# A list scheduler orders the second half of an output projection and the up stage, and activation sums are formed in place

## The chip, the cores and the metric

One Trainium2 chip, one of its cores. The time is that of one execution of the program on the device, in microseconds. The core's engines each run their own queue of instructions in order: TensorE (PE; its weight loads are PEld), VectorE (DVE), ScalarE (ACT), GpSimd (POOL), and SyncE (SP), which issues the DMAs.

## The reference

The kernel is one layer of a hybrid decoder block on 1024 positions of width 1024, all in float32: a gated DeltaNet and a sparse attention side by side, a gated merge of the two, and a gated feed-forward part with a depthwise convolution. What the change touches is the end:

```python
m      = sigmoid(gA) * (o_A @ W_A) + sigmoid(gB) * (o_B @ W_B)
h      = LayerNorm(alpha * x + m @ W_out)                # (1024, 1024)
u_g, u_v = split(causal_depthwise_conv3(h @ W_up))       # W_up: 1024 x 5632
f      = (silu(u_g) * u_v) @ W_down                      # W_down: 2816 x 1024
out    = LayerNorm(alpha * h + f)
```

## The kernel before, in words

**Precision.** Each float32 operand of a product is a sum of a high and a low part. The high part is a rounding copy on ACT, the low part the difference, formed on DVE or POOL. A product is high x high, high x low and low x high: three matmuls where one would stand.

**Output projection.** `merge(tt, nh)` computes 128 positions (row block `tt`, 0 to 7) by 512 columns (half `nh`): 24 matmuls into one PSUM bank (`pq`; there are eight). `mT` holds m transposed, high and low, for positions 0 to 511 and 512 to 1023: four tiles, which are the operands of the merges. After the merge, DVE adds alpha * x into `hS` and takes the statistics, POOL raises the variance to the power -1/2, DVE forms the shift, ACT normalises. Then a row block of the first half (tt 0 to 3) is scaled and shifted by four POOL sums (`ln_pool`), one of the second half (4 to 7) by four DVE sums out of PSUM (`ln_psum`, `ln_out`). Then it is stored to DRAM (`hres`), and transposed by eight PE instructions into two banks.

**Up stage.** h @ W_up is done as a 2 x 2 block product with seven products for eight (Strassen's form as Winograd has it). The blocks are positions 0 to 511 and 512 to 1023, depth 0 to 511 and 512 to 1023, and, for column group f (0 to 21), the 128 gate and the 128 value columns. `XB[n]` (n 1 to 7) are the seven sums of activations, high and low. `XB[1]` and `XB[2]` are the two depth halves of positions 0 to 511 (`turn_first`); 3, 5, 6, 7 and 4 come from positions 512 to 1023 and those (`turn_second`: ACT copies and high parts, DVE sums and low parts, POOL two low parts and a sum). They cannot start on a block before it is transposed. `make(f, n)` makes the weights of product n of group f: sums of the raw blocks on POOL, the high part on ACT, the low part on POOL. `Group.run(n)` is the product, 12 matmuls; `Group.after(n)` what follows on ACT and DVE: sums of products (`u`), the convolution's three taps into `accs`, and in `gate` the tanh form of silu and the product with the value half. The result is stored (`gdr`).

**What sets the order.** In this part of the program the order on every engine is the one in which the instructions are written (`manual_schedule`). The tiles of `XB[1]` and `XB[2]` take slots of a pool of six that the first projection half's weights free; `XB[3]`, 5, 6 and 7 take four that are free once the last merge has read `mT`. So the second half's sums start when all merges are over. Four groups (0 to 3) run products 1 and 2 ahead, one group between each of the transpositions 4 to 7, while the others are formed. From then on a table sets the steps: products 6, 7, 5, 4, 3 for the first four groups, 1, 6, 7, 5, 2, 4, 3 for the rest, weights made up to eight products ahead in a ring of ten tiles.

**Down stage.** For each half of the positions, four row blocks with two banks each. The first `KF` = 4 of 22 depth tiles go to row blocks 0 and 1, then to 2 and 3, so that the second pair of banks is wanted later; then tile by tile, and the last six row block by row block, each ending in the second LayerNorm.

Of the kernel before, what the change touches and what calls it, by code (L numbers as in the profile page):

```python
# [25 lines left out]
LNLAG = 2  # L26
# [24 lines left out]
def hybrid_block_kernel(ctx: ExitStack, tc: tile.TileContext, x, w_in, gdn_conv_w, gdn_a_log,  # L51
# [997 lines left out]
    def merge(tt, nh):  # L1049
        hf, o = tt // 4, (tt % 4) * 128  # L1050
        hs = HS[nh]
        who, wlo = wo[nh]
        ps = pq()
# [5 lines left out]
        V.scalar_tensor_tensor(hrow(tt)[:, hs], hrow(tt)[:, hs], ALPHA, ps, op0=OP.mult, op1=OP.add)  # L1059

    def turned(tt):
        ps = [pq(), pq()]
        for k in range(KT):
            PE.transpose(ps[k // 4][:, (k % 4) * 128:(k % 4 + 1) * 128], hrow(tt)[:, k * 128:(k + 1) * 128], ident)
        return [p.rearrange("p (k c) -> p k c", k=4) for p in ps]

    def turn_first(tt):
        o = slice(tt * 128, tt * 128 + 128)
        ps = turned(tt)
        for n, pv in zip((1, 2), ps):  # L1070
            A.activation(XB[n][:, 0, :, o], pv, AF.Copy)
        for n, pv in zip((1, 2), ps):
            V.tensor_tensor(XB[n][:, 1, :, o], pv, XB[n][:, 0, :, o].bitcast(F32), op=OP.subtract)

    def turn_second(tt):
        o = slice((tt - 4) * 128, (tt - 4) * 128 + 128)
        p12, p22 = turned(tt)

        def part(n, i):
            return XB[n][:, i, :, o]  # L1080

        def tmp():
            return ff.tile([128, 512], F32, name="tb", tag="tb", bufs=4).rearrange("p (k c) -> p k c", k=4)

        def hi(n, src):
            A.activation(part(n, 0), src, AF.Copy)

        def lo(n, src, eng):
            eng.tensor_tensor(part(n, 1), src, part(n, 0).bitcast(F32), op=OP.subtract)

        t3, t4 = tmp(), tmp()
        A.activation(t3, p12, AF.Copy)
        hi(3, p22)
        V.tensor_tensor(p12, p12, part(1, 0).bitcast(F32), op=OP.subtract)
        V.tensor_tensor(p12, p12, part(1, 1).bitcast(F32), op=OP.subtract)
        A.activation(t4, p12, AF.Copy)
        V.tensor_tensor(t3, p22, t3, op=OP.subtract)
        lo(3, p22, V)
# [5 lines left out]
        V.tensor_tensor(t4, p22, part(2, 0).bitcast(F32), op=OP.subtract)
# [342 lines left out]
```

## Time and profile before

| | us |
|---|---|
| median of 3 runs | 1816.57 (1814.01 to 1817.13) |
| the profiled execution | 1816.3 |
| its span in the profile | 1814.6 |
| PE busy in the span | 1720.6 (95%) |
| DVE, ACT, POOL busy | 1070.5, 726.1, 822.3 |
| PE busy in 1020 to 1200 us (180 us) | 127.94 |
| PE busy in 1200 to 1520 us (320 us) | 318.84 |

A row of a group gives the line in the kernel, engine, operation, output<-inputs, shape and count, then busy time and mean ns of one, then the time the engine stood idle just before such instructions and what ended it. A row of a timeline begins with the start and the duration in us; "x12" are twelve instructions merged into one row. The chain of waits is the work that ended last, followed back. All matmuls, of merges, products and the down stage, stand on one line (L97), and are told apart by their tiles: `woh`, `wol` with `mT` in the merges, `xb` with `wb` in the up stage, `wd` with `gs` in the down stage.

### The profile page before, as it was taken

Reading aid. Unit: us, or ns where it says so; the run is one execution under the profiler, and the core shown is the slowest. Engines: PE = TensorE matmul, PEld = TensorE weight load, DVE = VectorE, ACT = ScalarE, POOL = GpSimd, SP = SyncE. Lnnn points to the kernel's source line nnn. Section 1 sums busy time; section 2 is a strip of 40 time slices with the busy share of each in tenths; the row PEclk is TensorE's granted clock in tenths of the full one; section 3 lists DMA queues with packets and bytes.
Section 4 is the critical chain, followed back from the end, with each engine's and each line's share of the span. In section 5 each row is a group of like instructions: output and inputs, shape, how many; then the busy total and the mean of one; then the engine's idle time right before and its main releaser. Section 6 shows DMA issues by size and latency. Waiting matters only on the chain.

```text
span 1814.6 us, 23297 instructions
## 1 busy us (share of the span) xinstructions
PE 1720.6 (95%) x8710; PEld 1444.7 (80%) x8710; DVE 1070.5 (59%) x2048; ACT 726.1 (40%) x1282; POOL 822.3 (45%) x609
## 2 busy tenths in 40 slices
PE   8999999999999999999899965799999999899997
PEld 8888888888888788888687854578888888688886
DVE  3567767576625388898633264386666666613624
ACT  3323323222224488888531033244444444431421
POOL 1322222222214244444672244777777776654731
PEclk9999999999999999999999987899999999899999
DMA  5222122222213000000256021233223222763521
GB/s 168 71 83 61 45 69 56 58 60 72 83 47 96 25 1 1 1 1 7 87 186 232 12 93 47 59 104 92 71 82 93 81 82 99 285 225 110 175 92 47
DMA packets 158382, 152.38 MB, mean 84 GB/s; under 512 B 16392, under 2 KB 129213, under 8 KB 158269
## 3 DMA queue, kind: packets, MB, share of 16 engines
q1 hardware_dynamic: 158269, 150.89, 26.4%
q8 instruction: 69, 1.13, 0.3%
q14 instruction: 44, 0.36, 0.1%
HBM read 119.67 MB, written 31.20 MB: 83 GB/s over the span
## 4 chain that ended last, share of the span: by engine, by line
PE 83%; DVE 6%; POOL 4%; ACT 3%; issue 2%; DMA 1%; SPq 0%; POOLq 0%; DVEq 0%; ACTq 0%
PE pq L97 35%; PE big L97 32%; PE sm L97 12%; PE sm L852 3%; POOL wb L1173 1%; DVE accs L1193 1%; POOL h L1139 1%; POOL h L1138 1%; ACT P L817 1%; DVE gs L1374 0%; DVE st L815 0%; DMA w<-in_w_down_dram 0%; DVE wl L855 0%; ACT wb L1172 0%; POOL tb L1161 0%
## 5 line engine op out<-in xcount | busy, mean ns | idle before, releaser
L97 PE MATMUL pq<-xb,wb 128*128 128x512 f32 x1848 | 430.9, 395 | 48.4 <-ACT u L1216 37.8
L97 PEld LDWEIGHTS pq<-xb,wb 128*128 128x128 f32 x1848 | 352.3, 191 | 125.3 <-ACT u L1216 39.3
L87 POOL TENSOR_TENSOR wl<-w,wh 128x1024 fp32r<-128x1024 f32 (+2 forms) x51 | 122.5, 2407 | 361.4 <-PE big L97 130.2
L97 PE MATMUL big<-xTl,wh 128*128 128x512 f32 x624 | 249.9, 401 | 0.0
L97 PE MATMUL big<-xTh,wh 128*128 128x512 f32 x624 | 249.7, 400 | 0.0
L97 PE MATMUL pq<-wd,gs 128*128 128x512 f32 x1056 | 243.1, 392 | 6.1 <-DVE accs L1246 4.0
L97 PEld LDWEIGHTS pq<-wd,gs 128*128 128x128 f32 x1056 | 199.8, 189 | 49.1 <-DVE accs L1246 5.1
L1193 DVE SCALAR_TENSOR_TENSOR accs<-pq,fcw,accs 128x511 f32<-128x511 f32 (+3 forms) x264 | 144.9, 569 | 87.7 <-ACT accs L1196 83.2
L97 PE MATMUL big<-xTh,wl 128*128 128x512 f32 x624 | 163.7, 398 | 0.0
L779 POOL TENSOR_TENSOR P<-P,st 128x640 f32<-128x640 f32 (+7 forms) x96 | 99.8, 1067 | 126.6 <-DVE st L788 61.1
L1173 POOL TENSOR_TENSOR wb<-w,wb 128x512 fp32r<-128x512 f32 x88 | 113.2, 1293 | 80.4 <-ACT wb L1172 79.7
L1366 POOL TENSOR_TENSOR wd<-w,wd 128x1024 fp32r<-128x1024 f32 x44 | 110.7, 2537 | 70.5 <-ACT wd L1365 70.5
L97 PEld LDWEIGHTS big<-xTl,wh 128*128 128x128 f32 x624 | 117.6, 188 | 20.9 <-issue 0.2
L97 PEld LDWEIGHTS big<-xTh,wh 128*128 128x128 f32 x624 | 117.6, 189 | 20.8
L97 PEld LDWEIGHTS big<-xTh,wl 128*128 128x128 f32 x624 | 113.9, 188 | 22.0
L1196 ACT ACTIVATE accs<-pq,fcw 128x512 f32<-128x512 f32 x88 | 59.9, 684 | 163.1 <-PE pq L97 80.9
L1374 DVE TENSOR_TENSOR gs<-gr,gs 128x512 fp32r<-128x512 f32 x44 | 57.9, 1327 | 91.7 <-ACT gs L1373 91.6
L855 DVE TENSOR_TENSOR wl<-sm,wh 128x512 fp32r<-128x512 f32 (+1 forms) x148 | 99.6, 683 | 11.3 <-ACT wh L854 8.9
L86 ACT ACTIVATE wh<-w 128x1024 fp32r<-128x1024 f32 (+2 forms) x51 | 53.1, 1047 | 127.2 <-PE big L97 85.7
L854 ACT ACTIVATE wh<-sm 128x512 fp32r<-128x512 f32 (+1 forms) x148 | 87.1, 594 | 27.9 <-PE sm L852 24.1
L97 PE MATMUL big<-kS,qS 128*128 128x512 f32 (+3 forms) x384 | 89.0, 350 | 3.0 <-DVE qS L631 3.0
L817 ACT ACTIVATE P<-big,st 128x640 f32<-128x640 f32 (+7 forms) x128 | 88.6, 699 | 6.6 <-DVE st L815 6.1
(344 smaller groups left out, 3200.9 us busy)
## 6 DMA issues: line engine op xcount, KB each, us to landing
w<-in_w_down_dram SPq DMA_DIRECT2D x44, 512.0 KB, 3.8
w<-in_w_in_dram SPq DMA_DIRECT2D x40, 512.0 KB, 4.2
w<-in_w_up_dram SPq DMA_DIRECT2D x36, 512.0 KB, 3.9
gdr<-accs SPq DMA_DIRECT2D x22, 512.0 KB, 2.6
gr<-gdr SPq DMA_DIRECT2D x44, 256.0 KB, 3.6
sig<-th SPq DMA_DIRECT2D x32, 256.0 KB, 2.4
w<-sig SPq DMA_DIRECT2D x16, 512.0 KB, 3.3
wx<-in_w_up_dram SPq DMA_DIRECT2D x11, 512.0 KB, 5.2
```

The source lines that it names most:

```text
L87: G.tensor_tensor(wl[:, :n], w[:, :n], wh[:, :n].bitcast(F32), op=OP.subtract)
L97: PE.matmul(o, a, b, start=start, stop=stop, skip_group_check=True)
L779: G.tensor_tensor(p, p, r.to_broadcast([128, p.shape[1]]), op=OP.mult)
L817: A.activation(P[:, r0 + i, :n], pv[:, i], AF.Exp, bias=nm[:, i:i + 1], accum_out=su[:, i:i + 1])
L852: PE.transpose(tp[:n, r * 128:(r + 1) * 128], P[:, r, c0:c0 + n], ident)
L854: A.activation(ph, tp[:n], AF.Copy)
L855: V.tensor_tensor(pl, tp[:n], ph.bitcast(F32), op=OP.subtract)
L1173: G.tensor_tensor(w[:, 1], src, w[:, 0].bitcast(F32), op=OP.subtract)
L1193: V.scalar_tensor_tensor(o, i, fcw[:, 2 - s, j:j + 1], o, op0=OP.mult, op1=OP.add)
L1196: A.activation(acc[:, HS[h]], p, AF.Copy, scale=fcw[:, 2, j:j + 1])
L1366: G.tensor_tensor(o[:, 1], w, o[:, 0].bitcast(F32), op=OP.subtract)
L1374: V.tensor_tensor(g[:, 1], r, g[:, 0].bitcast(F32), op=OP.subtract)
```

## The change

A scheduler is added to the kernel: each piece of work is a node with an engine (or two to choose from, with a duration each), nodes that it depends on, and tokens that it takes and gives (banks, ring tiles, raw tiles, temporaries). PE's merges and products have a fixed order (`seq`); from their times each node gets a latest start; then time is stepped, each free engine taking the ready node with the earliest. The nodes are emitted in that order.

With it: the second half of the projection runs the row blocks as 0, 4, 1, 5, 2, 3, 6, 7; `XB[1]`, 2, 6 and 7 are the `mT` tiles themselves, a block's columns being overwritten when its merge has read them; the temporaries of the sums are a pool of 3 (before: 4), with one tile apart for a weight sum; the low parts of the weights of groups 0 to 2, and the weight sums of groups 0 and 1, may go to DVE; a row block of h is stored in one DMA instead of two; and `KF` is 6.

```diff
+class Plan:
+    LAT = {"PE": .25, "A": .15, "V": .15, "G": .15, "S": 1.6, "X": 0}
...
+            for e in free:
+                if free[e] > t + 1e-9:
+                    continue
+                for n in todo[e]:
...
+                    if any(d.end is None or d.end + d.lat > t + 1e-9 for d in n.deps):
+                        continue
+                    if any(len(self.pools[p]) < n.take.count(p) for p in n.take):
+                        continue
...
+                    n.start, n.dur = t, n.engs[e]
+                    n.end = free[e] = t + n.dur
...
-    def xblock(n, pool):
-        XB[n] = pool.tile([128, 2, 4, 512], F32R, name=f"xb{n}", tag="s")
+    for n, (q, hf) in {1: ("h", 0), 2: ("l", 0), 6: ("h", 1), 7: ("l", 1)}.items():
+        XB[n] = mT[q, hf].rearrange("p (i k) c -> p i k c", i=2)
+    for n in (3, 5):
+        XB[n] = S6.tile([128, 2, 4, 512], F32R, name=f"xb{n}", tag="s")
...
+    P.pool("bank", 8)
+    P.pool("ring", tokens=["wh", "wl", "wh", "wl"])
+    P.pool("raw", tokens=["w", "w", "w"])
+    P.pool("tmp", 3)
...
+    ORDER = (0, 4, 1, 5, 2, 3, 6, 7)
...
+        merged[tt] = P.add("PE", 5.45, m, [prev], take=["bank"], seq=True)
+        n = P.add("V", 2.3, st, [merged[tt]], take=["ag"], give=[(merged[tt], "bank")])
+        w = P.add("G", .5, lambda _: ln_pow(s["ag"]), [n])
+        w = P.add("V", .16, lambda _: ln_shift(s["ag"]), [w])
...
+        turned[tt] = P.add("PE", 1.05, t_, outs + [merged[tt]], take=["bank", "bank"], prio=-30)
...
+        D12 = add("V", 1.3, d12, [t, f1, A1])
+        A3 = add("A", .5, a3, [D12], take=["tmp"])
+        H5 = add("A", .5, hi(5, tt, p12), [D12])
+        D3 = add("V", .6, lambda _: V.tensor_tensor(t3(), p22(), t3(), op=OP.subtract), [A1])
...
+        L7 = add({"G": 1.25, "V": .65}, None, lo(7, tt, t3), [H7], give=[(A1, "tmp")])
...
+        L4 = add({"G": 1.25, "V": .65}, None, lo(4, tt, t4), [H4], give=[(A3, "tmp")])
...
+        fast = {"G": 1.25, "V": .65} if f < 3 else "G"
...
+        H = P.add("A", .53, h_, deps + [chain["make"]], take=["ring"], node=True)
...
+        L = P.add(fast, 1.25, l_, [H], give=list(give))
...
+            e = {"G": 1.25, "V": .65} if f < 2 else "G"
...
+            self.s1 = P.add(e, 1.25, s1, [w1, w2, chain["sum"]], take=["sum"], node=True)
+            self.s2 = P.add(e, 1.25, s2, [self.s1] + wait, take=["tmp"], node=True)
...
+            deps = [W[f, n][1]] + xdone[n] + ([] if free else [chain["prod"]])
+            deps += {2: [self.n.get("u1")], 4: [self.n.get("u2")], 3: [self.n.get("c22")]}.get(n, [])
+            p = self.n[n] = P.add("PE", 2.724, p_, deps, take=["bank"] if head else [],
+                                  give=[(W[f, n][0], "ring")], seq=True)
...
+    for g in groups[:AHEAD]:
+        g.run(1, True)
+        g.run(2, True)
...
+    order = P.run()
...
+        with tc.manual_schedule(engines=ME):
+            for n in part:
+                n.emit()
...
-    KL, KF = 6, 4
+    KL, KF = 6, 6
```

**PE, from the end of the merges to product 6 of group 0.** `h_9096` are row blocks 0 to 3, `h_9097` blocks 4 to 7; `x8` is one block's transposition; `mTh_8479` and `mTl_8480` are the mT tiles of the first half of the positions, in the changed kernel also `XB[1]` and `XB[2]`; `xb_9340` and `xb_9341` are `XB[1]` and `XB[2]` before. Before:

```order
L97 MATMUL pq<-xb_9340,wb 128x512 x12
L1064 MATMUL pq<-ident,h_9097 128x128 x8
L97 MATMUL pq<-xb_9341,wb 128x512 x12
L1064 MATMUL pq<-ident,h_9097 128x128 x8
L97 MATMUL pq<-xb_9340,wb 128x512 x12
L97 MATMUL pq<-xb_9341,wb 128x512 x12
L1064 MATMUL pq<-ident,h_9097 128x128 x8
```

And now, from the last matmul of merge 6 (the 23 matmuls between the first and the last of merge 7 are left out):

```order
L191 MATMUL pq<-woh_9322,mTl_8482 128x512
L1252 MATMUL pq<-ident,h_9096 128x128 x8
L1252 MATMUL pq<-ident,h_9097 128x128 x8
L191 MATMUL pq<-woh_9322,mTh_8481 128x512
...
L191 MATMUL pq<-woh_9322,mTl_8482 128x512
L1252 MATMUL pq<-ident,h_9096 128x128 x8
L191 MATMUL pq<-mTh_8479,wb 128x512 x24
L1252 MATMUL pq<-ident,h_9097 128x128 x16
L191 MATMUL pq<-mTl_8480,wb 128x512 x24
L191 MATMUL pq<-mTh_8479,wb 128x512 x24
L191 MATMUL pq<-mTl_8480,wb 128x512 x24
L191 MATMUL pq<-mTh_8481,wb 128x512 x12
```

Transpositions 2 and 5 stand between merges 6 and 7, 3 behind merge 7, 6 and 7 together behind two products; before, each of 4 to 7 had one or two products around it.

**DVE, from merge 7's residual to the low parts of block 3.** L1151 is the residual, L1177 to L1187 the statistics and the shift, L1309, L1311 and the `xb_9341` row pieces of block 5's sums, the last two rows the low parts of block 3 for `XB[1]` and `XB[2]`:

```order
L1151 SCALAR_TENSOR_TENSOR h_9097<-h_9097,pq 128x512
L1177 BN_STATS bs<-h_9097 128x6
L1187 SCALAR_TENSOR_TENSOR ag<-ag 128x1
L1309 TENSOR_TENSOR pq<-pq,tb 128x512
L1267 TENSOR_TENSOR xb_9341<-pq,xb_9341 128x4x128
L1177 BN_STATS bs<-h_9097 128x6
L1179 BN_AGGR ag<-bs 128x2
L1180 TENSOR_SCALAR ag<-ag 128x1
L1311 TENSOR_TENSOR tb<-pq,mTl_8480 128x512
L1267 TENSOR_TENSOR mTh_8479<-pq,mTh_8479 128x4x128
L1267 TENSOR_TENSOR mTl_8480<-pq,mTl_8480 128x4x128
```

Before, the low parts of block 3 stood behind merge 5's statistics, and merge 7's residual behind the four sums of row block 6.

**DVE, between the sums and group 0's first product sum.** Before, `u` (L1219) came directly behind the sums' low parts (L1089):

```order
L1089 TENSOR_TENSOR xb_9753<-pq,xb_9753 128x4x128
L1089 TENSOR_TENSOR xb_9752<-pq,xb_9752 128x4x128
L1219 TENSOR_TENSOR u<-pq,u 128x512
L1222 TENSOR_TENSOR u<-pq,u 128x512
L1224 TENSOR_TENSOR pq<-pq,u 128x512
```

Now there stand between them low parts and sums of weights (L1371, L1422, L1427) and the taps of groups 0 and 1 (L1382):

```order
L1267 TENSOR_TENSOR xb_9807<-tb,xb_9807 128x4x128
L1382 SCALAR_TENSOR_TENSOR accs<-pq,fcw,accs 128x510
L1371 TENSOR_TENSOR wb<-tb,wb 128x512
L1382 SCALAR_TENSOR_TENSOR accs<-pq,fcw,accs 128x511
L1371 TENSOR_TENSOR wb<-wx,wb 128x512
L1371 TENSOR_TENSOR wb<-sb,wb 128x512
L1382 SCALAR_TENSOR_TENSOR accs<-pq,fcw,accs 128x510
L1371 TENSOR_TENSOR wb<-w,wb 128x512
L1422 TENSOR_TENSOR tb<-sb,w 128x512
L1427 TENSOR_TENSOR w<-w 128x512
L1371 TENSOR_TENSOR wb<-tb,wb 128x512
L1480 TENSOR_TENSOR u<-pq,u 128x512
```

The weight rows were POOL's before; they have both operands in SBUF (`w`, `wx`, `tb`, `sb`, `wb`).

More of the change, by code (lines that the diff above doesn't have):

```diff
@@ L1058, in merge @@
             mm(ps, ml, who[:, k, :], False, k == KT - 1)
[L1059 to L1073, printed above, removed]
@@ new lines, in residual @@
+    def residual(ps, tt, nh):
+        o = hrow(tt)[:, HS[nh]]
+        V.scalar_tensor_tensor(o, o, ALPHA, ps, op0=OP.mult, op1=OP.add)
+    with tc.manual_schedule(engines=MS):
+        for tt in range(NT):
+            ps = pq()
+            merge(ps, tt, 0)
+            residual(ps, tt, 0)
+        for k in range(0, KT, 2):
+            load_out(1, k, wtile())
+    for n, (q, hf) in {1: ("h", 0), 2: ("l", 0), 6: ("h", 1), 7: ("l", 1)}.items():
+        XB[n] = mT[q, hf].rearrange("p (i k) c -> p i k c", i=2)
@@ new lines, in hybrid_block_kernel, with hi, lo, turn_first @@
+    for tt in ORDER:
+        rows(tt)
+    last_merge = merged[ORDER[-1]]
+    xdone = {n: [] for n in range(1, 8)}
+    def hi(n, tt, src):
+        return lambda _: copy(xpart(n, 0, tt), src())
+    def lo(n, tt, src):
+        return lambda e: e.tensor_tensor(xpart(n, 1, tt), src(), xpart(n, 0, tt).bitcast(F32), op=OP.subtract)
+    first = {}
+    def turn_first(tt):
+        s = state[tt]
+        for i, n in enumerate((1, 2)):
+            a = P.add("A", .5, hi(n, tt, lambda i=i: s["p"][i]), [turned[tt]])
+            first[tt, n] = P.add("V", .6, lo(n, tt, lambda i=i: s["p"][i]), [a], give=[(turned[tt], "bank")])
+            xdone[n].append(first[tt, n])
@@ L1178, in product, with tile_u, taps @@
+    def tile_u():
+        return ff().tile([128, 512], F32, name="u", tag="u", bufs=5)
+    def taps(acc, p0, p1, j, part, s):
+        o, i = {"0": (acc[:, s:512], p0[:, :512 - s]), "1": (acc[:, 512 + s:], p1[:, :512 - s]) if p1 is not None
+                else None, "s": (acc[:, 512:512 + s], p0[:, 512 - s:])}[part]
+        V.scalar_tensor_tensor(o, i, fcw[:, 2 - s, j:j + 1], o, op0=OP.mult, op1=OP.add)
+    def product(o, f, n, start, stop):
+        w = W[f, n][0].tile
         for k in range(4):
@@ new lines, in after @@
+                N["sa"] = scaled(0, "a", 0, f, [N[2], chain.get("acc", None)], take=["acc"])
+                N["ta"] = tap(0, "a", None, f, "0", [N["sa"]])
+                c = scaled(1, "c", 1, NFF + f, [N["c22"], N["sa"]])
+                c21 = P.add("V", .6, lambda _: V.tensor_tensor(t["b"], t["u3"], t["b"], op=OP.subtract), [p, N["u3"]],
+                            give=[(N["u3"], "u")])
+                b = scaled(1, "b", 0, NFF + f, [c21, N["sa"]])
+                x = tap(1, "b", "c", NFF + f, "1", [c], [(N[7], "bank")])
@@ new lines, in hybrid_block_kernel @@
+    groups = [Group(f) for f in range(NFF)]
+    for g in groups[:AHEAD]:
+        g.weights(0)
+    for f, g in enumerate(groups):
+        if f >= AHEAD:
+            g.weights(0)
+        g.weights(1)
+    for g in groups[:AHEAD]:
+        g.run(1, True)
+        g.run(2, True)
+    chain["prod"] = groups[AHEAD - 1].n[2]
+    for f, g in enumerate(groups):
+        for n in ([6, 7, 5, 4, 3] if f < AHEAD else [1, 6, 7, 5, 2, 4, 3]):
+            g.run(n)
+    order = P.run()
+    cut = next(i for i, n in enumerate(order) if n is opened)
```

537 lines of the change are left out of this document (311 added, 226 removed).

## The prediction, on record before the changed kernel was run

> **What bounds the kernel now.** I read the page's busy shares and chain first, then TensorE's groups stage by stage, then the places where it stood still.
>
> ```profile
> PE 1720.6 (95%) x8710; PEld 1444.7 (80%) x8710; DVE 1070.5 (59%) x2048; ACT 726.1 (40%) x1282; POOL 822.3 (45%) x609
> ...
> PE 83%; DVE 6%; POOL 4%; ACT 3%; issue 2%; DMA 1%; SPq 0%; POOLq 0%; DVEq 0%; ACTq 0%
> ```
>
> TensorE (PE) sets the end nearly everywhere; the 17% of the chain on other engines is what a reordering can win. These are groups of the windows 990 to 1200 us (two rows), 1200 to 1520 and 1500 to 1815:
>
> ```profile
> L97 PE MATMUL pq<-xb,wb 128*128 128x512 f32 x286 | 76.4, 429 | 47.3 <-ACT u L1216 37.8 <-DVE accs L1193 7.6 <-DVE pq L1224 1.3
> L1064 PE MATMUL pq<-ident,h 128*128 128x128 f32 x64 | 8.8, 275 | 4.8 <-DVE xb L1073 4.3 <-POOL h L1139 0.5
> L97 PE MATMUL pq<-xb,wb 128*128 128x512 f32 x1407 | 319.3, 389 | 1.2 <-DVE pq L1224 1.2
> L97 PE MATMUL pq<-wd,gs 128*128 128x512 f32 x1056 | 243.1, 392 | 6.1 <-DVE accs L1246 4.0 <-DVE accs L1193 2.1
> ```
>
> The up stage's products run without a gap from 1200 us on (319.3/1407 = 0.227 us per matmul, 2.72 us per product of 12); nearly all waiting lies in its first 286 matmuls. The changed stretch on PE, in time; brackets give the idle time before a row and what ended it:
>
> ```profile
> 1061.32 0.80 PE L97 MATMUL pq<-woh,mTh 128*128 128x512 f32 x1
> ...
> 1064.47 0.46 PE L97 MATMUL pq<-wol,mTh 128*128 128x512 f32 x1
> ...
> 1073.87 2.89 PE L97 MATMUL pq<-xb,wb 128*128 128x512 f32 x12
> ...
> 1092.02 4.54 PE L97 MATMUL pq<-xb,wb 128*128 128x512 f32 x12 [14.39 <-ACT u L1216]
> ...
> 1105.83 4.47 PE L97 MATMUL pq<-xb,wb 128*128 128x512 f32 x12 [5.63 <-ACT u L1216]
> ...
> 1123.22 4.32 PE L97 MATMUL pq<-xb,wb 128*128 128x512 f32 x12 [9.31 <-ACT u L1216]
> ...
> 1128.17 2.98 PE L97 MATMUL pq<-xb,wb 128*128 128x512 f32 x12
> 1139.63 20.94 PE L97 MATMUL pq<-xb,wb 128*128 128x512 f32 x84 [8.48 <-ACT u L1216]
> 1168.15 22.01 PE L97 MATMUL pq<-xb,wb 128*128 128x512 f32 x84 [7.58 <-DVE accs L1193]
> ```
>
> By the group rows PE stood idle 47.3 us before products and 4.8 before transpositions (L1064), 52.1 in all. After a long wait it is slow: between 1061.32 and 1064.47, behind the wait of 4.3, seven matmuls took 3.15 us instead of 1.59, 1.6 lost; the blocks of 12 behind a wait took 4.54, 4.47 and 4.32 instead of 2.89, 4.7 lost; the blocks of 84 took 20.94 and 22.01 instead of 19.2, 4.5 lost. Together **62.9 us** that a better order could win here.
>
> Why they arise shows in the chain: each transposed row block goes through ACT, DVE and POOL while PE's next product stands behind it in PE's own queue.
>
> ```profile
> 1025.47 0.69 DVE h L1059
> ...
> 1042.57 0.52 POOL ag L293
> 1043.31 1.25 ACT h L1136
> 1044.63 1.30 POOL h L1138
> 1046.00 1.29 POOL h L1139
> 1047.29 1.26 POOL h L1138
> 1048.62 1.27 POOL h L1139
> 1049.89 0.52 POOL ag L293
> ```
>
> One row block of the first half costs a POOL-paced 7.3 us (1042.57 to 1049.89) against 5.45 us for its merge on PE (24 x 0.227). Four in a row, as now, fall behind PE. A block of the second half uses DVE instead (four sums, 2.6 us at L1104's price below).
>
> **The change, part by part.**
>
> *Merges 0, 4, 1, 5, 2, 3, 6, 7 instead of 0 to 7.* Nothing is added on PE: the same 192 matmuls and 64 transposes. Alternation gives POOL two merges per expensive block for the first three. I followed the new queues with the rows above: merge 0 ends at 1025.2 (L1059 reads it at 1025.47); its rows are ready at 1035.2 as now, and PE reaches transposition 0 at 1036.1. Transpositions 4, 1, 5, 2 and 3 have rows ready at about 1042.4, 1046.5, 1056.6, 1060 and 1067.4, and PE comes at 1042.7, 1049.2, after 1061, 1061 and 1068.7. No wait; the smallest margins, 0.3 and 0.9 us, may each cost a few tenths.
>
> *Sums in place over mT.* This is what allows it: XB1, 2, 6 and 7 need no tile that only frees after the last merge, so the second-half sums of blocks 4 and 5 are formed during the merges. It adds no instruction.
>
> *First product after transposition 3.* Here I find a new wait. DVE's queue holds, between the end of merge 7 and the low part of XB1 for block 3, merge 7's residual and statistics, a shift and three pieces of block 5. Their prices:
>
> ```profile
> 1069.05 1.29 DVE L1073 TENSOR_TENSOR xb<-pq,xb 128x512 fp32r<-128x512 f32 x2 [2.07 <-ACT xb L1071]
> ...
> 1080.22 1.28 DVE L1114 BATCH_NORM_STATS2 bs<-h 128x6 f32<-128x512 f32 x2
> ...
> 1088.78 0.69 DVE L1104 TENSOR_TENSOR tb<-pq,xb 128x512 f32<-128x512 f32 x1 [0.66 <-ACT xb L1086]
> ```
>
> 0.2 hop, 0.6 residual, 1.2 statistics, 0.6 for three tiny rows, three sums at 0.65, one low part 0.6: 5.2 us, of which the transposition covers 0.9. PE waits 4.3 us, and as after the 4.3 us of now loses 1.6 more to the clock. Bounds: 2 us, if the hops overlap, to 6.
>
> *Products 1 and 2 of four groups, with transpositions 6 and 7 between them in one place.* The four pairs no longer stand behind one transposition each: what PE did between 1073.87 and 1131.1 in pieces is 8 x 2.72 = 21.8 us in one run. Block 7 leaves DVE about 0.4 us after PE wants it: 0.4.
>
> *Weight sums and low parts on DVE for the first three groups.* The plan prices such a row at 0.65 us on DVE. The trace does not: with both operands in SBUF and POOL working beside it, DVE was slower, with one operand in PSUM it was not. (The first row gives min/median/max in ns.)
>
> ```profile
> L1374 DVE TENSOR_TENSOR gs<-gr,gs x44: 670/890/2892, 1535.4 to 1751.0; 128x512 fp32r<-128x512 f32 x44
> L919 DVE TENSOR_TENSOR oAl<-gA,oAh 128x512 fp32r<-128x512 f32 x4 | 5.4, 1385 | 0.0
> L855 DVE TENSOR_TENSOR wl<-sm,wh 128x512 fp32r<-128x512 f32 x132 | 89.0, 684 | 8.6 <-ACT wh L854 6.6
> L1173 POOL TENSOR_TENSOR wb<-w,wb 128x512 fp32r<-128x512 f32 x88 | 113.2, 1293 | 80.4 <-ACT wb L1172 79.7
> ```
>
> I take 1.3 us per such row while POOL is at its own sums (bounds 0.67 and 1.55; L919 is nearest, since POOL's rows are 1.3 us there too). [...]
>
> Where that falls: count from the end of transposition 7. PE has 6 products before group 0's product 6, so it comes to product 4 of group 0 after 9 x 2.72 = 24.5 us. Product 4 needs DVE's u2. In DVE's queue ahead of it stand 17 sums of blocks 6 and 7 (11.1 us at 0.65), 9 two-SBUF rows (11.7), 4 taps (2.6) and u2 itself (0.7) with hops (0.8): 27 us. PE waits **2.5**, then 0.4 for the sum that frees bank d. The backlog of some 6 us passes to group 1, whose product 5 needs group 0's bank b: **3.3**. I add 0.9 for the clock. [...] Groups 2 and 3 then have DVE free enough: a group needs
>
> ```profile
> 1200.00:1520.00 320.00, 318.84 (x1407) 263.74 (x1406) 214.20 (x362) 138.35 (x237) 234.44 (x186) 1.00 0.27 84
> ```
>
> (columns: PE, PE load, DVE, ACT, POOL) 214.2 x 19.05/320 = 12.8 us of DVE against 13.6 of PE with five products.
>
> *Groups 4 to 21.* Ring of ten weight tiles, makes per group, lead and the order of loads and gate stores are as before within one instruction. I price it at 0: PE's own 19.05 us per group cover POOL's 14.2 (11 rows at 1.29) and DVE's 12.8. Three temporaries for four and one sum tile cost nothing as long as POOL's chain stays inside that.
>
> *Down stage, six tiles first instead of four.* Now:
>
> ```profile
> 1558.60 8.77 PE L97 MATMUL pq<-wd,gs 128*128 128x512 f32 x38
> 1569.51 1.38 PE L97 MATMUL pq<-wd,gs 128*128 128x512 f32 x3 [2.14 <-DVE accs L1193]
> 1574.85 25.41 PE L97 MATMUL pq<-wd,gs 128*128 128x512 f32 x100 [3.96 <-DVE accs L1246]
> 1561.76 1.06 ACT L1365 ACTIVATE wd<-w 128x1024 fp32r<-128x1024 f32 x1 [5.05 <-DMA w<-in_w_down_dram]
> ```
>
> PE runs out of banks until the last group's gate is through (6.1 us), then is slow (25.41 for 100 against 22.9: 2.5). Two more tiles on the first two row blocks are 24 matmuls, 5.45 us of other work in that wait. Their loads pass through the same ACT queue in which the gate's scaling already stood behind a load (the 5.05), so the gate may come later by as much: bounds 0 and 8.6. I take 5.5.
>
> *Tail.* The last row block's chain is the same instructions: 0.
>
> **Sum.** Lost now 62.9. Lost after: 4.3+1.6+0.4+2.5+0.4+3.3+0.9 = 13.4. Won 49.5 here and 5.5 in the down stage, 55. The profiled execution took 1816.3 us (span 1814.6 and 1.7 around it; the runs' median is 1816.57, 0.3 above): 1816.3 - 55 = **1761**.
>
> [...]
>
> **The rivals.**
>
> - *DVE and POOL hardly collide* (POOL often waits for ACT): only the wait after transposition 3 stays, 62.9 - 6.3 + 5.5 = 62 won, 1754. For it: POOL stood idle 79.7 us for ACT in the L1173 row. Against: in this stretch POOL has its own backlog.
> - *DVE becomes the bound of the first four groups.* 12.8 of 13.6 us leaves it nothing to catch up with, and groups 1 and 2 still get two-SBUF rows; groups 2 and 3 then lose some 5.5 each, and the result is 1772.
> - *Slower:* the weight chain bounds groups 4 to 21. With one sum tile, a group's first sum waits for the last one's two-term weights; POOL's 14.2 us and the ACT hops between its rows would have to come to more than 19.05 + 55/18 = 22.1 us per group to turn the gain into a loss; at 23, 1761 + 18 x 3.95 = 1832. Against: now the same rows fit, with PE idle 1.2 us in 320.
> - *The change doesn't move what waits.* The queues show that it does: one product pair per transposition before, none after.
>
> **How the numbers follow.** My forecast 0.48, no collision 0.20, DVE bound 0.24, slower 0.05, no change 0.03. The least that the bounds give is 1749 (no collision, 8.6 in the down stage), the most of the first three about 1778 (waits at their upper bounds, nothing in the down stage). The range 1750 to 1777 holds them and leaves out the last two and the tails. A measurement of this kernel can tell 0.2% (3.6 us) from no change; faster 0.93, same 0.02, slower 0.05.
>
> **What would show it.** Right: PE without a wait over 1 us from merge 0 to transposition 3; one of some 4 us before the first product, ended by DVE's low part of XB1; waits of 2 to 4 us in groups 0 and 1, ended by DVE; two-SBUF rows of DVE at 1 us or more there; PE gapless from group 4 on; about 4 us less idle at the first bank wait of the down stage. Wrong: a transposition late by several us, gaps in every group after the fourth, or the first down tiles late on PE ahead of the last two products.

## The result, and the profile after

The changed kernel takes 1762.66 us (median of four runs, 1758.11 to 1763.04) where the kernel before takes 1816.11 on the same chip: 0.9701 of the time, 95% interval 0.9683 to 0.9720. The forecast was 1761, with a range of 1750 to 1777. The profiled execution took 1762.67 us. From its page, the busy shares, the chain of waits and three groups of PE:

```profile
PE 1719.1 (98%) x8710; PEld 1440.8 (82%) x8710; DVE 1100.4 (62%) x2068; ACT 732.2 (42%) x1282; POOL 804.8 (46%) x589
...
PE 85%; DVE 6%; issue 3%; ACT 2%; POOL 2%; DMA 1%; DVEq 0%; POOLq 0%; ACTq 0%; SPq 0%
...
L191 PE MATMUL pq<-wd,gs 128*128 128x512 f32 x1056 | 241.5, 391 | 0.4 <-DVE accs L1513 0.4
...
L191 PE MATMUL pq<-xb,wb 128*128 128x512 f32 x792 | 189.0, 393 | 2.6 <-DVE accs L1382 2.1
...
L191 PE MATMUL pq<-mTh,wb 128*128 128x512 f32 x528 | 127.3, 397 | 3.2 <-ACT mTh L1172 3.1
```

The products now read `mTh` and `mTl` as well as `xb`, since four of the seven sums lie there. Before, 47.3 us of idle time stood ahead of the products; now 2.6 and 3.2. All that PE waits for between 1000 and 1200 us (engine, tile and line of the waiting row, what it waited for, us in total, times, longest):

```profile
PE pq L191 <- ACT mTh L1172: 3.1, 1, 3.1
PE pq L191 <- DVE accs L1382: 2.1, 1, 2.1
PE pq L191 <- DVE pq L1485: 0.5, 1, 0.5
PE pq L1252 <- DVE h L1241: 0.3, 1, 0.3
```

In the windows view (PE, PE load, DVE, ACT, POOL, clock) PE is without a gap from 1145 to 1500 us:

```profile
1145.00:1500.00 355.00, 355.00 (x1559) 292.40 (x1558) 234.16 (x398) 160.12 (x264) 253.12 (x197) 1.00 0.27 86
```

In the timeline, two blocks behind waits show the slow clock, and the last row is the down stage, 330 matmuls without a wait:

```profile
1078.36 8.73 PE L191 MATMUL pq<-mTh,wb 128*128 128x512 f32 x24 [3.08 <-ACT mTh L1172]
...
1127.55 10.03 PE L191 MATMUL pq<-xb,wb 128*128 128x512 f32 x36 [2.10 <-DVE accs L1382]
...
1514.75 75.42 PE L191 MATMUL pq<-wd,gs 128*128 128x512 f32 x330
```

At 0.227 us each, and 0.16 more for the last, 24 matmuls take 5.6 us and 36 take 8.3; so 3.1 and 1.7 us went to the clock.

**A measure that leaves out what comes before.** Three tiles mark three points: `woh` the first matmul of the projection, `wb` the last product of the up stage, `wd` the last of the down stage (duration min/median/max in ns, then first and last start). Before, and after:

```profile
L97 PE MATMUL pq<-woh,mTh x128: 389/389/796, 976.2 to 1073.2; 128*128 128x512 f32 x128
L97 PE MATMUL pq<-xb,wb x1848: 387/389/796, 1073.9 to 1558.4; 128*128 128x512 f32 x185
L97 PE MATMUL pq<-wd,gs x1056: 388/389/796, 1550.2 to 1804.3; 128*128 128x512 f32 x176
```

```profile
L191 PE MATMUL pq<-woh,mTh x128: 387/389/496, 982.0 to 1073.6; 128*128 128x512 f32 x128
L191 PE MATMUL pq<-xb,wb x792: 388/389/628, 1110.8 to 1514.5; 128*128 128x512 f32 x198
L191 PE MATMUL pq<-wd,gs x1056: 388/389/503, 1504.1 to 1750.8; 128*128 128x512 f32 x176
```

From the first projection product to the last up product it was 582.2 us and is 532.5 (49.7 won); from there to the last down product 245.9 and 236.3 (9.6 won). But the first projection product comes 5.8 us later than before: 49.7 + 9.6 - 5.8 + 0.1 of the tail = 53.6, the difference of the two profiled executions (1816.3 - 1762.67). (Some 2 us of down products have moved ahead of the last up product, 10.4 us of overlap against 8.2, so the border between the first two numbers is soft by that much.) The same three points in all profiles of this study, one profile per kernel (the last column is the median of several runs; the kernel before, run beside each batch, had medians of 1814.78 to 1816.12):

| kernel | first projection product at | to last up product | to last down product | median of the runs |
|---|---|---|---|---|
| before | 976.2 | 582.2 | 245.9 | 1816.11 |
| changed | 982.0 | 532.5 | 236.3 | 1762.66 |
| changed, again | 980.2 | 532.6 | 236.3 | 1761.14 |
| late sums | 980.2 | 533.4 | 239.3 | 1764.71 |
| rows in turn | 979.6 | 534.1 | 237.0 | 1761.99 |
| KF 4 | 982.5 | 532.7 | 242.2 | 1766.32 |
| weights on POOL only | 982.3 | 529.4 | 236.3 | 1757.15 |
| block 3 first | 980.9 | 532.1 | 236.6 | 1761.23 |
| POOL only and block 3 first | 981.0 | 532.7 | 236.4 | 1760.76 |
| three freedoms taken back | 978.8 | 531.9 | 237.4 | 1760.23 |
| and PE's queue as before | 977.6 | 534.2 | 239.8 | 1765.05 |
| before, product 1's copy first | 974.3 | 568.4 | 243.3 | 1799.78 |
| and scaling ahead of weights | 975.7 | 566.8 | 244.5 | 1799.20 |
| before, KF 6 | 974.8 | 583.8 | 236.8 | 1808.74 |

### The profile page after: what moved, and what is told of

It is laid out like the page before. It is cut to its first block, busy times and chain, and to the rows that moved or that the text cites. A ratio compares the mean times of both kernels' runs of the same rounds, so it can differ in the third digit from the quotient of the medians.

```text
span 1761.0 us, 23301 instructions
## 1 busy us (share of the span) xinstructions
PE 1719.1 (98%) x8710; PEld 1440.8 (82%) x8710; DVE 1100.4 (62%) x2068; ACT 732.2 (42%) x1282; POOL 804.8 (46%) x589
## 3 DMA queue, kind: packets, MB, share of 16 engines
q8 instruction: 69, 1.13, 0.3%
## 4 chain that ended last, share of the span: by engine, by line
PE 85%; DVE 6%; issue 3%; ACT 2%; POOL 2%; DMA 1%; DVEq 0%; POOLq 0%; ACTq 0%; SPq 0%
PE pq L191 35%; PE big L191 33%; PE sm L191 13%; PE sm L946 3%; ACT P L911 1%; DVE st L909 1%; DVE wb L1371 1%; DVE accs L1382 0%; DVE wl L949 0%; POOL h L1228 0%; POOL h L1229 0%; DMA w<-in_w_out_dram 0%; PE big L245 0%; DVE gs L1573 0%; DVE oAl L1013 0%
## 5 line engine op out<-in xcount | busy, mean ns | idle before, releaser
L191 PE MATMUL pq<-xb,wb 128*128 128x512 f32 x792 | 189.0, 393 | 2.6 <-DVE accs L1382 2.1
L1382 DVE SCALAR_TENSOR_TENSOR accs<-pq,fcw,accs 128x510 f32<-128x510 f32 (+3 forms) x264 | 145.8, 569 | 63.3 <-ACT accs L1466 58.1
L191 PEld LDWEIGHTS pq<-xb,wb 128*128 128x128 f32 x792 | 149.7, 189 | 35.6 <-ACT wb L1172 2.5
L191 PE MATMUL pq<-mTh,wb 128*128 128x512 f32 x528 | 127.3, 397 | 3.2 <-ACT mTh L1172 3.1
L191 PE MATMUL pq<-mTl,wb 128*128 128x512 f32 x528 | 127.4, 391 | 0.0
L191 PEld LDWEIGHTS pq<-mTh,wb 128*128 128x128 f32 x528 | 100.8, 191 | 25.7 <-ACT mTh L1172 3.3
L1371 POOL TENSOR_TENSOR wb<-w,wb 128x512 fp32r<-128x512 f32 x79 | 102.8, 1302 | 37.8 <-ACT wb L1172 37.8
L191 PEld LDWEIGHTS pq<-mTl,wb 128*128 128x128 f32 x528 | 99.1, 188 | 21.2
L1573 DVE TENSOR_TENSOR gs<-tb,gs 128x512 fp32r<-128x512 f32 x44 | 71.4, 1641 | 67.0 <-ACT gs L1572 64.2
L949 DVE TENSOR_TENSOR wl<-sm,wh 128x512 fp32r<-128x512 f32 (+1 forms) x148 | 99.8, 684 | 13.7 <-ACT wh L948 11.3
```

The costliest lines, as they stand in the source:

```text
L191: PE.matmul(o, a, b, start=start, stop=stop, skip_group_check=True)
L949: V.tensor_tensor(pl, tp[:n], ph.bitcast(F32), op=OP.subtract)
L1371: e.tensor_tensor(H.tile[:, 1], src(), H.tile[:, 0].bitcast(F32), op=OP.subtract)
L1382: V.scalar_tensor_tensor(o, i, fcw[:, 2 - s, j:j + 1], o, op0=OP.mult, op1=OP.add)
L1573: V.tensor_tensor(g[:, 1], r, g[:, 0].bitcast(F32), op=OP.subtract)
```

## The experiments

**The kernel again.** Nothing edited.

> The changed kernel once more, unedited. In its first profile the output projection's first product began at 981.99 us, 5.8 us later than before's (976.16), after a stretch from 880 to 900 us in which the granted clock was 0.66 and 0.83 where before had 0.99 and 1.00, though the code up to there is the same. Theory: that delay belongs to the run and not to the change, so another execution may begin the projection between 976 and 982, and its time is between 1757 and 1763. Rival: the change itself delays this stretch (its code or buffers lie elsewhere); then the first product begins at 982 again within 1 us.

1761.14 us (1759.48 to 1762.88), ratio 0.9704 (0.9688 to 0.9720). From the first projection product to the last up product ("the stretch" from here on) it repeats to 0.1 us. The projection began at 980.2 us, which by the bounds set above is the theory and not the rival. But the table has fourteen profiles: without the scheduler the projection begins at 974.3 to 976.2 (four), with it at 977.6 to 982.5 (ten). The two groups do not overlap, although ahead of the projection every engine's instructions are the same ones in the same order. So it is not only the run, as I had it; what in the change causes it, no run tells.

**Sums behind the last merge.**

```diff
+        after = last_merge
...
-        A1 = add("A", .5, a1, [t], take=["tmp"])
-        H3 = add("A", .5, hi(3, tt, p22), [t])
+        A1 = add("A", .5, a1, [t, after], take=["tmp"])
+        H3 = add("A", .5, hi(3, tt, p22), [t, after])
```

> The sums of row blocks 4 to 7 may start only after the last merge; all else stays. Theory: blocks 4 and 5 have their sums done beneath the merges in the changed kernel; put behind them, they give DVE about 2 blocks x 10 rows x 0.65 = 13 us more behind the last merge, where DVE is nearly full (26.9 of 30 us from 1070 to 1100), so the products that need the second half come 8 to 13 us later and 1 to 3 us go to the clock: 1771 to 1779. Rival: the eight products 1 and 2 that go first (8 x 2.72 = 21.8 us of TensorE) cover this; then the time stays within 2 us of the changed kernel's.

1764.71 us, ratio 0.9726 (0.9712 to 0.9741), 0.9 us more in the stretch, and 3.0 more in the down stage, for which I have no reason. The theory, 8 to 13, is wrong: the products 1 and 2 of four groups cover the sums. The rival, within 2 us, holds for the stretch; the whole is 2.1 and 3.6 us above the two medians of the changed kernel. That the sums can be formed during the merges was, by the prediction, what allowed the gain; in the stretch it is worth about 1 us.

**Row blocks in turn.**

```diff
-    ORDER = (0, 4, 1, 5, 2, 3, 6, 7)
+    ORDER = (0, 1, 2, 3, 4, 5, 6, 7)
```

> The row blocks are merged in the order 0 to 7 instead of 0, 4, 1, 5, 2, 3, 6, 7. Blocks 0 to 3 are normalised by POOL (4 rows x 1.29 = 5.2 us each) and 4 to 7 by DVE (4 rows x 0.69 = 2.8 us each, and 10 rows of sums). Theory: the interleaving is what keeps both engines level with a merge of 5.45 us; in turn, POOL is full for four blocks while DVE waits, and DVE then has four blocks of about 12 us one behind the other, which ends some 6 to 15 us later than now: 1768 to 1778. Rival: the order hardly matters, since TensorE's merges bound both halves: within 2 us of the changed kernel.

1761.99 us, ratio 0.9708 (0.9694 to 0.9723), 1.6 us more in the stretch and the whole as before the edit. The theory of 6 to 15 falls. PE's waits are more and shorter, none over 2.2 us.

**KF back to 4, and KF 6 alone in the kernel before.**

```diff
-    KL, KF = 6, 6
+    KL, KF = 6, 4
```

> Four products instead of six of the first pair of the down stage run ahead (KF 4, as before). Theory: the 7.9 us saved at the start of the down stage come from the two more products of 2 x 1.9 us that fill the waits for banks, so 5 to 8 us come back: 1767 to 1771. Rival: it was the order of the last groups' sums, which frees the banks earlier; then 0 to 2 us.

> The kernel before with KF 6 instead of 4 and nothing else. The changed kernel with KF 4 took 5.2 us more. Theory: the same 24 matmuls fill the same waits here, 4 to 6 us won: 1809 to 1811. Rival: in before the first waits of the down stage stand behind the loads of its first tiles, which wait for slots that the last groups still hold; then it is within 2 us of before.

KF 4 in the changed kernel: 1766.32 us, ratio 0.9734 (0.9719 to 0.9748), just below the theory's 1767; 5.9 us more behind the last up product. The waits for banks are back, in its timeline:

```profile
1526.68 0.97 PE L191 MATMUL pq<-wd,gs 128*128 128x512 f32 x3 [2.94 <-DVE accs L1513]
1528.01 62.18 PE L191 MATMUL pq<-wd,gs 128*128 128x512 f32 x264 [0.36 <-DVE accs L1513]
```

KF 6 alone in the kernel before: 1808.74 us, ratio 0.9959 (0.9945 to 0.9974), 7.3 us less than before's 1816.02 beside it, where 4 to 6 were expected; in the down stage it is 9.1 us less (245.9 to 236.8). There its down stage runs on without any wait:

```profile
1558.78 31.42 PE L97 MATMUL pq<-wd,gs 128*128 128x512 f32 x136
```

So this number alone is enough to save the time in the down stage. It is not the only way: the changed kernel with KF 4 has 242.2 us there, 3.7 less than before's 245.9. The loads that come ahead of the gate in ACT's queue, for which I had allowed up to 5 us, cost nothing that shows.

**All weight rows on POOL.**

```diff
-        fast = {"G": 1.25, "V": .65} if f < 3 else "G"
+        fast = "G"
...
-            e = {"G": 1.25, "V": .65} if f < 2 else "G"
+            e = "G"
```

> The sums and low parts of weights all go to POOL, as before the change; in the plan as it is, 17 of the rows that may go either way are DVE's and would now be POOL's. Theory: 17 rows of 1.29 us are 22 us more for POOL while DVE gives up about 17 x 1.1; POOL has 46 us idle in 1020 to 1145, but the rows are wanted within the first three groups, so 4 to 12 us are lost against the changed kernel: 1766 to 1774. Rival: the collision of the two engines costs as much as the help brings (DVE rows at 1.1 to 1.8, POOL rows at 1.64 to 1.75 instead of 1.29); then it is level or 2 to 4 us faster: 1758 to 1762.

1757.15 us, ratio 0.9679 (0.9665 to 0.9694): the rival, a little below even its 1758, and the lowest median here. The ratio's interval still overlaps the changed kernel's, so the whole time does not settle it; but the stretch is 3.1 us shorter, where the unedited kernel repeats to 0.1, and the 2.1 us wait for bank b is gone. Groups of the window 1090 to 1145, in the changed kernel:

```profile
L1371 POOL TENSOR_TENSOR wb<-wx,wb 128x512 fp32r<-128x512 f32 x3 | 4.3, 1421 | 2.0 <-ACT wb L1172 1.9
L1371 DVE TENSOR_TENSOR wb<-sb,wb 128x512 fp32r<-128x512 f32 x3 | 4.3, 1417 | 0.0
L1422 POOL TENSOR_TENSOR tb<-sb,w 128x512 f32<-128x512 f32 x2 | 3.5, 1731 | 0.0
L1371 DVE TENSOR_TENSOR wb<-w,wb 128x512 fp32r<-128x512 f32 x3 | 3.2, 1070 | 0.0
...
L1371 DVE TENSOR_TENSOR wb<-tb,wb 128x512 fp32r<-128x512 f32 x3 | 2.5, 841 | 0.1
L1371 DVE TENSOR_TENSOR wb<-wx,wb 128x512 fp32r<-128x512 f32 x2 | 2.5, 1232 | 0.0
```

and with POOL alone:

```profile
L1371 POOL TENSOR_TENSOR wb<-w,wb 128x512 fp32r<-128x512 f32 x9 | 11.6, 1291 | 0.0
L1371 POOL TENSOR_TENSOR wb<-sb,wb 128x512 fp32r<-128x512 f32 x4 | 5.2, 1298 | 0.0
```

A low part of weights takes DVE 1.13 us on average in eleven rows (4.3 + 3.2 + 2.5 + 2.5 us), not the 0.65 of the plan, while POOL's rows become 1.42 and 1.73 instead of 1.29. (Not every slow POOL row comes from the help: with POOL alone, too, one row of L1422 takes 1.74, beside DVE's own low parts of the activations.) Alone, POOL works without idle time in these groups and is in time. The help held up taps that PE was waiting for. Both engines pay here: beside POOL's rows, from 1102.84 to 1109.3 us, DVE's rows with both operands in SBUF took 1.12, 1.13, 1.79 and 1.34 us, and the next three, while POOL stood idle (1108.77 to 1111.27), 0.68, 0.68 and 0.69; in the means of these groups a POOL row was 0.43 us at most above the 1.30 of its low parts without the help.

**Block 3 ahead of norm 6, and this with POOL alone.** In the changed kernel ACT's queue at the first product was:

```profile
1075.83 1.49 ACT L1190 ACTIVATE pq<-h,ag 128x512 f32<-128x512 f32 x2 [0.75 <-DVE ag L1187]
1077.25 1.05 ACT L1172 ACTIVATE mTh<-pq 128x512 fp32r<-128x512 f32 x2
```

```diff
-                z = P.add("A", .72, z_, [w], take=["bank"], ...)
+                z = P.add("A", .72, z_, [w] + ([turned[3]] if tt == 6 else []), take=["bank"], ...)
...
-            a = P.add("A", .5, hi(n, tt, ...), [turned[tt]])
+            a = P.add("A", .5, hi(n, tt, ...), [turned[tt]], prio=-40 if tt == 3 else 0)
```

(and the same `prio` for the two low parts on DVE.)

> In the changed kernel ACT normalises row block 6 only when transposition 3 is through, and the two copies of block 3 and DVE's two low parts of it go ahead of all else there. Theory: the wait of 3.1 us ahead of the first product is norm 6 (1.49 us) and one weight row standing ahead of the copies; it falls to about 1.5, and of the 3.1 us lost to the clock after it most goes: 3 to 5 us faster than the changed kernel, 1757 to 1759. Rival: norm 6 coming later moves the wait to transposition 6: no change within 1.5 us.

1761.23 us, ratio 0.9697 (0.9683 to 0.9712): as the changed kernel. Its timeline on PE:

```profile
1074.98 0.49 PE L191 MATMUL pq<-mTh,wb 128*128 128x512 f32 x1 [0.85 <-ACT mTh L1172]
1077.54 7.14 PE L191 MATMUL pq<-mTh,wb 128*128 128x512 f32 x23 [2.06 <-DVE mTh L1267]
```

The wait for the copy falls from 3.08 to 0.85 us, and now the second matmul waits 2.06 us for the low part on DVE, the wait that the prediction had named; in the changed kernel it was covered by the ACT copy. Block 6, held back, then makes its transposition wait. One place was three waits deep.

> The two edits of the changed kernel together that looked useful: all weight rows on POOL, and block 3's copies and low parts ahead of norm 6 and of all else. Theory: the first took away the wait of 2.1 us for bank b and the slow clock after it (3.1 us less up to the last up product), the second only turned one wait of 3.1 and its slow clock into five short ones; together 528 to 530 from the first projection product to the last up product, 1755 to 1759 in all. Rival: they share one wait, and the shorter waits at the transpositions delay the weights: 1760 to 1763.

1760.76 us, ratio 0.9697 (0.9684 to 0.9710): the rival. The two edits do not add up: the stretch takes 532.7 us, and POOL alone had 529.4. The transpositions of the last blocks wait four times, 3.0 us in all (2.3 with block 3 first alone), and the 24 matmuls behind them take 7.64 us where 5.6 is usual:

```profile
1088.89 7.64 PE L191 MATMUL pq<-mTl,wb 128*128 128x512 f32 x24
```

So POOL alone paid in one kernel and not in this one.

**The copy of product 1 ahead of the sums, in the kernel before.** By now neither the order of the rows nor the early sums had explained 50 us. In before, ACT's queue between the first two products was, from 1082 us on:

```profile
1082.86 1.48 ACT L1126 ACTIVATE pq<-h,ag 128x512 f32<-128x512 f32 x2 [5.23 <-DVE ag L1119]
1084.28 0.57 ACT L1092 ACTIVATE tb<-pq 128x512 f32<-128x512 f32 x1
1084.76 0.58 ACT L1086 ACTIVATE xb<-pq 128x512 fp32r<-128x512 f32 x1
1086.35 0.60 ACT L1096 ACTIVATE tb<-pq 128x512 f32<-128x512 f32 x1 [1.02 <-DVE pq L1095]
1086.94 0.63 ACT L1086 ACTIVATE xb<-tb 128x512 fp32r<-128x512 f32 x1
1088.15 1.08 ACT L1086 ACTIVATE xb<-pq 128x512 fp32r<-128x512 f32 x2 [0.57 <-DVE pq L1101]
1090.85 0.63 ACT L1086 ACTIVATE xb<-tb 128x512 fp32r<-128x512 f32 x1 [1.62 <-POOL tb L1107]
1091.39 0.58 ACT L1216 ACTIVATE u<-pq 128x512 f32<-128x512 f32 x1
```

Product 1 had ended at 1076.8 (1073.87 + 2.89). Its copy `u`, which product 2 waits for, ran 14.6 us later. Ahead of it stood norm 7, which itself waited 5.23 us for DVE, and then seven rows of block 4's sums, some of which waited for DVE and POOL; each part held the copy up by some 7 us.

```diff
         g0.run(1)
-        turn_second(4)
-        ln_out(hrow(7), ps, g1h, b1h, done)
         g0.after(1)
+        turn_second(4)
+        ln_out(hrow(7), ps, g1h, b1h, done)
         g0.run(2)
...
-        turn_second(5)
         g1.run(1)
-        make(3, 1)
-        make(3, 2)
         g1.after(1)
+        turn_second(5)
+        make(3, 1)
+        make(3, 2)
         g1.run(2)
```

(groups 2 and 3 in the same way.) In groups 1 to 3 the edit also moves product 1 itself ahead of the next transposition in PE's queue; in group 0 PE's order stays, and only the copy moves.

> The kernel before, with nothing of the change but one move: in each of the first four groups product 1 and ACT's copy u of it are written ahead of the sums of a row block instead of behind them; product 2 stays behind. In before, 37.8 of the 47.3 us idle ahead of products end with this copy. Theory, formed after the first four runs had shown that row order and early sums matter little: the copy was late because it stood in ACT's queue behind the copies of the sums, and with it PE's next transposition and so the next block's sums; moved ahead, the four blocks' sums follow each other at DVE's 6.5 us instead of at 13 to 17 us (L1094 at 1084.89, 1097.66, 1111.47, 1128.70), the last ends near 1113 to 1116 instead of 1134.5, and 20 to 28 us are won against before: 1787 to 1795. Rival: the sums themselves are the bound (POOL's rows, the hops between three engines), the copy only happens to be what comes last; then under 8 us are won: above 1807.

1799.78 us, ratio 0.9913 (0.9897 to 0.9930): 16.2 us won, 13.8 in the stretch, between theory and rival. The longest waits of PE then:

```profile
PE pq L97 <- DVE accs L1193: 13.9, 1, 13.9
PE pq L97 <- ACT u L1216: 13.7, 4, 7.2
```

The waits for `u` fall from 37.8 to 13.7, but one of 13.9, for a tap, stands behind them where 7.6 stood. In group 0 the wait falls from 14.39 to 7.24 us by the copy's move alone; what is left of it is norm 7, which still goes ahead.

**And the scaling ahead of the weights.** That wait ended with a tap, which had waited 16.4 us for ACT's scaling L1196, which stood in ACT's queue behind copies of weights that wait for POOL.

```diff
-                if nmade < min(len(steps), i + LEAD + 1):
+                if nmade < min(len(steps), i + (4 if i < 10 else LEAD) + 1):
```

> The kernel before with product 1 and its copy ahead of the sums, as in the run before (1799.8), and with ACT's copies of weights written at most 4 instead of 8 products ahead for the first ten products. In that run the longest wait, 13.9 us, ended with a tap (L1193) that had waited 16.4 us for ACT's scaling (L1196), which stood behind six weight copies that wait for POOL's sums. Theory: it is again a row that could go behind rows that cannot; with two copies ahead of it instead of six, the scaling comes some 9 us earlier and 6 to 10 us are won against 1799.8: 1790 to 1794. Rival: POOL's rows are the bound (16 us per group with hops against 13.6 of TensorE), and less lead makes the weights late instead: no better than 1798.

1799.20 us, ratio 0.9916 (0.9902 to 0.9929): no gain on the run before, as the rival has it. The waits:

```profile
PE pq L97 <- ACT u L1216: 13.6, 4, 7.2
PE pq L97 <- DVE pq L1224: 4.3, 1, 4.3
...
PE pq L97 <- ACT pq L1243: 4.2, 1, 4.2
PE pq L97 <- DVE accs L1193: 2.5, 1, 2.5
```

The 13.9 did become 2.5, as the theory says of the scaling; two later waits of 4.3 and 4.2 took about half of it. PE waits 32.1 us in all between 1000 and 1200 instead of 37.6, but only 1.6 of these 5.5 us show in the stretch; the rest went to slow matmuls, such as 48 behind the wait of 4.3 that took 13.81 us where 11.1 is usual. Removing one blocked row uncovers the next.

**Three freedoms taken back together.** Rows in turn, sums behind the last merge, weights on POOL alone (the three diffs above).

> The changed kernel with three of its freedoms taken back at once: row blocks in the order 0 to 7, the sums of blocks 4 to 7 only after the last merge, all weight rows on POOL. What stays of the change ahead of the down stage is that every engine's queue is written by the scheduler. Theory: of the 49.7 us won between the first projection product and the last up product (582.2 in before, 532.5 now) nearly all is queue order, no row standing ahead of one that could go; then this stretch takes 530 to 540 and the whole 1758 to 1768. Rival: each of the three was replaced by the other two when it alone was taken back; together they are what the gain rests on; then the stretch takes over 550, the whole over 1778.

1760.23 us, ratio 0.9702 (0.9689 to 0.9715), 531.9 us in the stretch where the changed kernel has 532.5. None of the three, and not all together, carries the gain.

**And PE's queue as it was.** The three edits stay taken back, and added dependencies give PE the order of before; product 1 of group 0 alone ran one merge earlier.

```diff
+    for f, g in enumerate(groups[:AHEAD]):
+        first, second, back = (g.n[1], turned[4], g.n[2]) if f == 0 else (turned[4 + f], g.n[1], g.n[2])
+        P.extra += [(second, first), (back, second)] + ([(turned[5 + f], back)] if f + 1 < AHEAD else [])
```

> The kernel with the three freedoms taken back (rows 0 to 7, sums behind the last merge, weights on POOL; 531.9 us from the first projection product to the last up product), and now PE's queue too is what it was before the change from the last merges on: product 1 of group 0, transposition 4, product 2, transposition 5, the pair of group 1, transposition 6, the pair of group 2, transposition 7, the pair of group 3, then group after group. Left of the change there are the queues of ACT, DVE and POOL, and KF 6. Theory: these three queues are the cause; transposition 7 comes some 5 us later than in the run without this edit (about 1097 against 1091.9) and the sums behind it with it, of which part is covered: the stretch takes 533 to 542, the whole 1761 to 1770. Rival: the order on PE is the cause (one transposition per pair holds up the next block's sums, as the waits of before look); then at least half of the 50 us comes back: the stretch over 555, the whole over 1783.

1765.05 us, ratio 0.9725 (0.9704 to 0.9745), 534.2 in the stretch: the theory. PE has, from the last merges on, one transposition per pair of products again, and 48.0 of the 50.3 us between 582.2 and 531.9 stay won (the down stage has 2.4 us more than the run before it). The one difference left on PE, product 1 of group 0 ahead of merge 7, gives its copy up to one merge, 5.45 us, more time, far less than the 48. PE's longest waits, and the copy `u` of product 1 of group 0, which ran as soon as ACT was through with norm 6 and not behind a block's sums:

```profile
PE pq L193 <- ACT u L1174: 5.6, 3, 3.0
PE pq L193 <- DVE pq L1488: 2.3, 2, 1.3
PE pq L193 <- ACT wb L1174: 2.0, 1, 2.0
```

```profile
1072.11 0.60 ACT L1174 ACTIVATE u<-pq 128x512 f32<-128x512 f32 x1
```

## Why the prediction was right, and where it was not

Two rows for the points below: transpositions 6 and 7, then DVE's `u2` of group 0, in the changed kernel's timeline.

```profile
1086.93 2.10 PE L1252 MATMUL pq<-ident,h 128*128 128x128 f32 x16
...
1111.23 0.68 DVE L1480 TENSOR_TENSOR u<-pq,u 128x512 f32<-128x512 f32 x1
```

**The sum.** Lost after: 3.1 + 2.1 + 0.5 + 0.3 = 6.0 us idle and 3.1 + 1.7 of slow clock, 10.8, against 13.4 in the forecast. So 62.9 - 10.8 = 52.1 were won where 49.5 stood, and of the 59.3 us won behind the first projection product (828.1 to 768.8) 7.2 fall to the down stage, where 5.5 stood. The sum was 4.3 us too cautious, and the 5.8 us that the projection begins later, of which no term spoke, took it back. That 1761 was met within 2 us is partly this balance, and so partly luck.

- *No wait from merge 0 to transposition 3.* Right: one of 0.3.
- *4.3 us ahead of the first product, ended by DVE's low part.* The place is right, the wait is 3.1 and ended by ACT's copy, since norm 6 went ahead of it. I had followed DVE's queue and not ACT's. The low part was next, as the run with block 3 first shows. The clock after it took 3.1, not 1.6.
- *2.5 us for u2.* It did not come. From the end of transposition 7 to the end of `u2` DVE took 22.9 us (1089.0 to 1111.9), not 27, and PE needs 24.5. The failed term is mainly the price of 1.3 for a row with two SBUF operands: the nine such rows behind the sums took 1.04 on average (0.68 to 1.79), 9.4 us instead of 11.7. The hops, for which 0.8 stood, did not show: the queue had no idle time.
- *0.4 for bank d, 3.3 for bank b.* 0.5 and 2.1, with 1.7 of clock where 0.9, an estimate, stood. The longer waits for u2 and bank b that the 1778 of the bounds counts, no run of the changed kernel shows.
- *Groups 4 to 21 at 0, tail at 0.* Right: PE is gapless from 1145 to 1500 us; 10.3 us from the last down product to the end before, 10.2 after.
- *5.5 us in the down stage.* The cause is right, the size low; KF alone is worth 5.9 here and 9.1 in the kernel before.

**The step that failed is the reason for the gain.** The prediction counted rightly what could be won, and gave it to the wrong parts: the alternating rows, the sums in place "that allow it", and the pairs that no longer stand behind a transposition each on PE. Rows, early sums and DVE's help taken back together cost nothing (531.9), and PE's old queue, but for one product, put back on top of that costs 2.3 us (534.2). What is left of the change in that kernel is the order in the queues of ACT, DVE and POOL, and smaller things that no run put back: the tiles of the sums in place, the pool of temporaries, the single store of a row block. So that the queues carry the gain is shown by taking the other parts away, and in part directly: in the kernel before, moving product 1 and its copy ahead by hand won 13.8 us. PE's waits ended with `ACT u`, and I read them as PE being held up by its own queue. In fact every engine was waiting. The same window, 1070 to 1145, in before:

```profile
ACT tb L1092 <- PE pq L1064: 14.0, 3, 5.1
...
DVE pq L1094 <- ACT tb L1092: 25.8, 4, 11.4
...
POOL xb L1089 <- ACT xb L1086: 26.7, 8, 7.4
```

ACT waits for PE's transposition, DVE for ACT, POOL for ACT, and PE for an ACT row that could have run 14 us earlier. The scheduler puts a row into a queue only when, by its clock, nothing that the row needs is missing; with that the circle is gone on all engines at once (in this window DVE's waits sum to 31.0 us before and to 6.1 in the changed kernel, POOL's to 43.8 and 20.1), while by hand one blocked row after the other had to be found. How much of the rest of the 50 us each single queue carries was not separated.

**The rivals.** That DVE and POOL hardly collide is wrong (1.13 us for a low part of weights on DVE, not 0.65), and the conclusion drawn from it as well: the wait for bank b went away when POOL had all the work, not by DVE helping freely. DVE as the bound of four groups, and POOL's chain as the bound of the rest, did not show.

## What to carry to other kernels

When a wait ends with a short row on an engine that is not busy, look in that engine's queue for what stands ahead of the row, and on what that waits; a circle of waits over four engines looks, from PE, like a dependency. Removing one such row tells little about the total, since the next one stands behind it: order all queues of the stage together. And a helper engine has to be priced with what it does to the one that it helps: here 0.65 us in the plan was 1.13 in the trace, the helped engine's rows grew by up to 0.43 in the mean of a group, and without the help the stretch was 3.1 us shorter in one kernel and no shorter in another.

## What the hardware showed that I had not expected

**The clock after a wait.** After 3.08 us without work the granted clock (the number behind POOL's) was at half speed from 1078 to 1084 us, which cost 3.1 us; after 2.10 us it was 0.65 and 0.50 from 1128 to 1132, which cost 1.7. One stretch of the changed kernel:

```profile
1080.00:1082.00 2.00, 2.00 (x7) 1.52 (x5) 0.65 (x2) 1.68 (x4) 2.00 (x3) 0.50 0.00 0
```

Two kernels with the same two waits of 0.85 and 2.05 us around one matmul differ: 23 matmuls took 7.14 us with block 3 first, and in the kernel that has POOL alone as well they took 5.55, where 5.4 is usual (23 x 0.227 + 0.16):

```profile
1077.17 5.55 PE L191 MATMUL pq<-mTh,wb 128*128 128x512 f32 x23 [2.05 <-DVE mTh L1267]
```

There four matmuls of a transposition still took 0.66 us at 1085.46, and the slow rows came later, at and behind the waits of the transpositions: four took 1.12 us at 1086.80 and again at 1088.12, and 24 matmuls took 7.64 us (the row under "Block 3 ahead of norm 6"). From 1020 to 1145 us the granted clock was 0.97 there on average, and 0.99 with block 3 first alone. So the second kernel did not escape the slow clock; it had it later.

Why equal waits were followed by the slow clock at different times, no run shows.

**A later start of the projection.** Ten profiles of kernels with the scheduler begin the projection at 977.6 to 982.5 us, four without it at 974.3 to 976.2, with the same instructions in the same order ahead of it. A part of it is clock: in the three slices of 10 us from 870 to 900 the granted clock was 1.00, 0.66 and 0.83 in the changed kernel's profile, and 0.84, 0.99 and 1.00 in before's. The later start takes back about 5 us of the gain, and its cause stays open.
